# Retention and gated attention with their outputs made channels on partitions, normed by sums over partitions

## The chip, the cores and the metric

The kernel runs on one core of a Trainium2 chip. The metric is the device time of one execution in microseconds (us). TensorE (PE) multiplies; its weight loads are listed apart (PEld). VectorE (DVE), ScalarE (ACT) and GpSimd (POOL) do the elementwise work, and SP, ACT and POOL can issue DMAs.

## The reference, cut to what matters

`x` is 1024 tokens by 1024 channels in f32, and there are two layers. Each projects the normed and modulated `x` to 3088 columns, which are shared out to three groups of heads:

```python
(aq, ak, av, ag, rq, rk, rv, rg, gq, gk, gv, gg, ga) = jnp.split(proj, IN_SPLITS, axis=-1)
a_out = sliding_window_attention(aq, ak, av, sinks) * jax.nn.silu(ag)
r = retention(rq, rk, rv)                        # 4 heads of 64, chunks of 128 tokens
r_out = rms_norm(r) * jax.nn.silu(rg)            # normed over the 64 channels of each head
g = gated_linear_attention(gq, gk, gv, log_a)    # 4 heads, keys of 32, values of 64; log_a from ga
g_out = rms_norm(g, gla_norm_gain) * jax.nn.silu(gg)
y = jnp.concatenate([a_out, r_out, g_out], axis=-1) @ w_out
x = x + gate * rms_norm(y, post_gain)
```

Both recurrent groups work chunk by chunk. With scores `sc` (masked and decayed products of queries and keys) the output of a chunk is `sc @ v`, the part within the chunk, plus `q @ state`, the part from earlier chunks; then `state = decay * state + k^T @ v`.

## The kernel before

Tokens are cut into 8 tiles of 128, handled as `NP_` = 4 pairs. A projection must be as exact as f32, so weights and activations are kept as a high and a low fp32r part, and `accum` sums three products of parts over 8 slices of the 1024 channels: 24 products for a projection. `project` has the activations of one token tile as the stationary operand and up to 272 columns of weights moving, so its result has tokens on partitions. Products of intermediate data (scores, states, transposes) are plain f32, each of which the profile lists as two records.

The input weights come in units of 256 columns, in the order of the table `UNITS`, from DRAM over staging tiles to the arenas; `gg` comes first and carries the 16 columns of `ga`. SP issues most of the DMAs; the letters in `EN` say which engine does a step or issues a DMA (S for SP, A for ACT, G or P for POOL, V for DVE).

A layer runs in this order. `do_gates` projects `gg` and `rg` of each pair, makes SiLU of them (`silu2`: tanh on ACT, one DVE operation) and stores them to DRAM (`sgS`, `srS`). The projections of `ga` go to the job `gla_logits`. Then for each pair of tiles `rq`, `rk` and `rv` are projected and `ret_core` runs; then, in the same manner, gated attention's `gqk`, `gv` and `gla_core`; then attention; then the output projection, which reads the mixed outputs back from `mixS` in DRAM.

In both cores the output of a tile, `po`, has tokens on partitions and 4 heads by 64 columns. The part from the state is a product with 128 stationary columns (the queries), and within the chunk the scores of a head are stationary (128 by 128) and its 64 columns of values move. Then `head_norm_gate` (L988 to L1000) squares `po` on ACT (L990), sums 64 columns per head on DVE, raises to the power of -1/2 in `rstd_of` on POOL (L529), multiplies by it and by the gate on DVE (L995 and the next), has TensorE transpose the two halves (L176), and `store_mix` copies them as high and low parts and stores these to `mixS`.

Only TensorE's order is set by the program itself. Chains of steps are generators, called jobs. `job` starts one, `yield lat(key, l)` says that its next TensorE step may be issued so many microseconds later by a planner's clock `clk`, and `pump`, called between the products of projections, issues the steps that are due; flags such as `("stG", l, t)` carry a time from one job to another. The latencies stand in the table `L` (`hn1` is that from squares to transposes; a name with `@1` is that of layer 1). TensorE runs its instructions in this order whatever the real times are. A scheduler orders the other engines by data and free buffers. Buffers are the pools `t2` (512 columns, `B2` = 12), `t1` (256 columns, `B1` = 8), small ones, and in PSUM `mm` with 3 banks for projections and `aux` with 5 for all the rest. Names in the lists below are these pools' (`t`, `aux`, `mm`), with numbers of a buffer.

The profile shows helpers by their own lines: `mult` is L161, `transp` L176, ACT's copies L145, DMAs L150. L491 makes the low part of a weight, L624 to L628 the high and low parts of the normed input `hT`.

## Time and profile before

| what | us |
|---|---|
| median of 3 runs | 971.86 (971.38 to 972.01) |
| the profiled execution | 971.16 |
| its span from first to last instruction | 969.4 |
| PE busy | 951.3 |
| PEld busy | 829.4 |
| DVE busy | 640.2 |
| ACT busy | 410.1 |
| POOL busy | 272.5 |

The mean granted clock of TensorE was 0.996 of full speed. Times in the rows of the profile are microseconds from the span's start. Busy time counts an instruction from its start to its end, and ends of products on PE are modelled, so one product overlaps the next in the list; the distance from start to next start is what a product costs TensorE.

### The profile page before, as it was taken

The page shows a single profiled execution, that of the slowest core. Times are in us where ns is not written, and L with a number is a line of the kernel's source. Part 1 is how long each engine was busy: PE and PEld are TensorE (multiplying, and loading weights), DVE is VectorE, ACT ScalarE, POOL GpSimd, SP SyncE. Part 2 cuts the span into 40 slices and gives each one's busy share as a digit, 9 for nine tenths or more (in the row PEclk, how much of TensorE's full clock was granted, in tenths as well). Part 3 has the DMA queues.
Part 4 walks back from the last instruction along what each step waited for, and adds up shares of the span by engine and source line. Part 5 has one row for each costly group of instructions (what it writes and reads, how often), then busy time and mean ns, then how long its engine had stood idle before and what let it go on. Part 6 is the DMA issues. An engine that isn't in the chain of part 4 may idle for free.

```text
span 969.4 us, 18061 instructions
## 1 busy us (share of the span) xinstructions
PE 951.3 (98%) x6513; PEld 829.4 (86%) x6513; DVE 640.2 (66%) x1525; ACT 410.1 (42%) x1119; POOL 272.5 (28%) x323
## 2 busy tenths in 40 slices
PE   6999999999999999999999999999999999999997
PEld 1799999989998877878889999998999887777886
DVE  6886857777777777655586485686776577763332
ACT  2777312354422666622455531134652166761111
POOL 3243011533430344511242110144423034441000
PEclk9999999999999999999999999999999999999999
DMA  9943314624335355677455160253222333555871
GB/s 313 320 146 110 111 56 129 187 77 112 115 102 150 98 168 180 218 242 237 172 166 172 50 180 22 83 155 92 80 86 77 120 88 105 158 174 174 261 238 65
DMA packets 124293, 140.30 MB, mean 145 GB/s; under 512 B 12734, under 2 KB 95528, under 8 KB 124204
## 3 DMA queue, kind: packets, MB, share of 16 engines
q1 hardware_dynamic: 116204, 127.43, 42.9%
q10 hardware_dynamic: 8000, 11.72, 3.4%
q8 instruction: 51, 0.84, 0.4%
q14 instruction: 38, 0.31, 0.1%
HBM read 102.42 MB, written 34.60 MB: 141 GB/s over the span
## 4 chain that ended last, share of the span: by engine, by line
PE 86%; DMA 7%; DVE 3%; issue 2%; POOL 1%; ACT 0%; SPq 0%; DVEq 0%; ACTq 0%; POOLq 0%
PE mm L161 67%; PE aux L161 15%; PE aux L176 4%; DMA wm<-in_w_mod_dram 2%; DMA t<-in_x_dram 1%; DMA st<-in_w_in_dram 1%; DMA xk<-in_x_dram 1%; DMA t<-aoS 1%; DMA st<-in_w_mod_dram 1%; POOL sm L529 1%; DVE acc L367 0%; DVE t L1292 0%; POOL arena L491 0%; DVE t L624 0%; DMA c_ident<-cst_ident_dram 0%
## 5 line engine op out<-in xcount | busy, mean ns | idle before, releaser
L161 PE MATMUL mm<-arena,arena 128*128 128x256 f32 (+2 forms) x1896 | 303.0, 315 | 1.4 <-ACT arena L628 0.7
L161 PE MATMUL mm<-arena 128*128 128x256 f32 (+2 forms) x1824 | 294.7, 317 | 0.0
L161 PEld LDWEIGHTS mm<-arena,arena 128*128 128x128 f32 x1896 | 261.8, 188 | 24.6 <-ACT arena L628 1.2
L161 PEld LDWEIGHTS mm<-arena 128*128 128x128 f32 x1824 | 255.4, 191 | 22.0 <-issue 1.2
L161 PE MATMUL mm<-arena,mx 128*128 128x512 f32 (+1 forms) x744 | 168.7, 386 | 0.0
L161 PEld LDWEIGHTS mm<-arena,mx 128*128 128x128 f32 x744 | 135.6, 188 | 29.1 <-issue 1.5
L529 POOL TENSOR_TENSOR sm<-sm,mhalf 128x4 f32<-128x4 f32 (+1 forms) x60 | 51.8, 863 | 294.8 <-DVE sm L528 285.3
L491 POOL TENSOR_TENSOR arena<-st,arena 128x512 fp32r<-128x512 f32 x55 | 80.3, 1467 | 91.3 <-ACT arena L145 34.7
L145 ACT ACTIVATE t<-aux 128x512 f32<-128x512 f32 (+1 forms) x96 | 48.7, 521 | 106.4 <-PE aux L176 44.9
L943 POOL TENSOR_TENSOR smx<-smx,sm 128x512 f32<-128x512 f32 x32 | 36.2, 1131 | 114.8 <-DVE sm L942 111.4
L491 DVE TENSOR_TENSOR arena<-st,arena 128x512 fp32r<-128x512 f32 x65 | 62.3, 969 | 4.7 <-PE mm L161 2.6
L145 ACT ACTIVATE arena<-st 128x512 fp32r<-128x512 f32 x82 | 48.5, 626 | 29.0 <-PE mm L161 13.0
L1247 ACT ACTIVATE t<-mm 128x512 f32<-128x512 f32 x30 | 17.9, 597 | 92.2 <-PE mm L161 40.3
L939 ACT ACTIVATE smx<-smx,sm 128x129 f32<-128x129 f32 x128 | 50.0, 393 | 14.0 <-DVE sm L936 13.9
L1248 DVE TENSOR_TENSOR t<-mm,modg 128x512 f32<-128x512 f32 x30 | 20.6, 689 | 48.6 <-ACT t L1247 48.5
L367 DVE SCALAR_TENSOR_TENSOR acc<-st,c_act,acc 128x512 f32<-128x512 f32 x60 | 47.3, 788 | 7.5 <-DMA st<-in_w_mod_dram 6.8
L1292 DVE SCALAR_TENSOR_TENSOR t<-t,sm,t 128x512 f32<-128x512 f32 x32 | 25.9, 846 | 39.7 <-DMA t<-xs 20.8
L176 PE MATMUL aux<-c_ident,t 128*128 128x128 f32 x288 | 45.5, 278 | 2.9 <-DVE t L602 2.9
L176 PEld LDWEIGHTS aux<-c_ident,t 128*128 128x128 f32 x288 | 34.9, 144 | 7.3 <-DVE t L602 4.2
L934 DVE COPY_PREDICATED smx<-c_curmask,aux 128x256 f32<-128x256 int32 x64 | 25.5, 447 | 15.0 <-ACT smx L145 10.4
L990 ACT ACTIVATE t<-aux 128x256 f32<-128x256 f32 x32 | 12.2, 382 | 54.1 <-PE aux L161 26.8
L995 DVE TENSOR_TENSOR t<-aux,sm 128x256 f32<-128x256 f32 x32 | 13.6, 425 | 30.8 <-POOL sm L529 30.8
(214 smaller groups left out, 1300.9 us busy)
## 6 DMA issues: line engine op xcount, KB each, us to landing
st<-in_w_in_dram SPq DMA_DIRECT2D x96, 256.0 KB
st<-in_w_mod_dram SPq DMA_DIRECT2D x64, 256.0 KB
mx<-mixS SPq DMA_DIRECT2D x30, 512.0 KB
mixS<-t SPq DMA_DIRECT2D x64, 128.0 KB
st<-in_w_out_dram SPq DMA_DIRECT2D x32, 256.0 KB
mixS<-t SPq DMA_DIRECT2D x32, 256.0 KB
wm<-in_w_mod_dram SPq DMA_DIRECT2D x12, 512.0 KB
t<-in_x_dram SPq DMA_DIRECT2D x24, 256.0 KB
```

Source lines behind the costliest of these rows:

```text
L145: A.activation(dst, src, AF.Copy)
L161: T.matmul(dst, lhsT, rhs, start=start, stop=stop)
L176: T.transpose(dst, src, idn)
L367: V.scalar_tensor_tensor(acc, wt, c_act[:, k:k + 1], acc, ALU.mult, ALU.add)
L491: i = (G if first == 0 and kc in LOG else V if first == 0 else eng(f"wlo{kc}")).tensor_tensor(wt[:, 1, 2 * kc:2 * kc + 2, 0:256], st, f(hi ...
L529: after[2] = G.tensor_tensor(r, r, mhalf[:, :w], ALU.pow)
L934: V.copy_predicated(sv, curmask.unsqueeze(1).to_broadcast((P, 2, P)), pv[:, :, n // P - 1, :])
L939: A.activation(sm[:, h, :], sm[:, h, :], AF.Exp, bias=mx[:, h:h + 1], accum_out=sums[:, h:h + 1])
L943: eng("pn").tensor_tensor(sm[:, :, 0:128], sm[:, :, 0:128], rs.unsqueeze(2).to_broadcast((P, 4, P)), ALU.mult)
L1247: A.activation(yg, pm, AF.Square, accum_out=ss[:, nh:nh + 1])
L1248: V.tensor_tensor(yg, pm, modg[l][:, 512 * nh:512 * nh + 512], ALU.mult)
L1292: V.scalar_tensor_tensor(xt[j], yg[j], r, xt[j], ALU.mult, ALU.add)
```

## The change

Outputs, gates and norms of retention and gated attention are made with channels on partitions.

- `rv` takes the first place of `gg` among the units, and with it the 16 columns of `ga`. The values are projected in `do_gates`, stored to a new DRAM buffer `vS` by SP, and loaded back (`lv`, on ACT's queue) when `rq` of the tile is projected. `gg` is projected where `rv` was.
- `project_P` projects the gates with 128 channels of the weights stationary and the 256 tokens of a pair moving; the SiLU of a pair is one tile of 512 columns, stored and loaded as such.
- `within` makes the part within the chunk with the 64 value columns of a head stationary and the scores moving. A head's result takes 64 partitions, two heads fill the two halves, and the four heads and two tiles of a pair fill one PSUM bank `po` [128, 512]. All of it comes ahead of the parts from the state, which have the state stationary and the queries moving, in two products of 128 by 128 per tile.
- `head_norm_gate` runs once per pair. ACT squares and makes the high part (`sqh`), POOL subtracts for the low part (`sql`), two products with the block matrix `bones` (ones where row and column belong to the same head) sum over partitions into `pz`, ACT takes Ln and Exp of -1/2 of it, DVE multiplies with the gate and with `po` (L1007), and the high and low parts are stored. No transposes, no sums on DVE and no powers on POOL are left in it.
- Among the constants `B2` goes from 12 to 13, `B1` from 8 to 9, the low part of `hT` in layer 0 (`hlo0`) from POOL to DVE, `LOG` (weight slices whose low part POOL makes for the first unit) from `(0,)` to `(0, 1, 3)`, and `DH`, `RE` and `FIN`, numbers that place steps of the modulation and the first normed input, from 1 to 0. The table `L` is set anew: `hn1`, now from squares to sums, 8.14 to 4.0 and 10.35 to 4.07 in layer 1; `hn2` 3.76 to 10.19 and 3.59 to 9.0; `rc1` 0.73 to 6.0; `gc5@1` 1.38 to 0.05; `gc4@1` 1.87 to 0.05; and others by less.

```diff
-    ("gg", GG), ("rg", RG),
-    ("rq", RQ), ("rk", RK), ("rv", RV),
+    ("rv", RV), ("rg", RG),
+    ("rq", RQ), ("rk", RK), ("gg", GG),
...
-    sgS = dr.tile([NT, P, 256], F32, name="sgS")
-    srS = dr.tile([NT, P, 256], F32, name="srS")
+    sgS = dr.tile([NP_, P, 512], F32, name="sgS")
+    srS = dr.tile([NP_, P, 512], F32, name="srS")
+    vS = dr.tile([NT, P, 256], F32, name="vS")
...
+    def project_P(pm, l, p, w):
+        h = hT[(l, p)]
+        for t in (2 * p, 2 * p + 1):
+            await_flag(("hT", l, t))
+        for j in range(2):
+            accum(pm[:, 256 * j:256 * j + 256], lambda a, k: w[:, a, k, j * P:j * P + P], lambda b, k: h[:, b, k, 0:256])
...
-    def store_mix(t, kt0, src, n):
...
+    def within(po, i, v, sc):
+        for j in range(2):
+            for r in range(2):
+                h = 2 * j + r
+                mult(po[64 * r:64 * r + 64, 256 * j + P * i:256 * j + P * i + P], v[:, 64 * h:64 * h + 64], sc[:, h],
+                     not i and not j, False, 0.108)
+
+    def head_norm_gate(l, p, po, gate, scale, eps, kt0):
+
+        sq, sh, sl = t2(), t2(F32R), t2(F32R)
         A.activation(sq, po, AF.Square)
-        ss = small(4)
-        V.tensor_reduce(ss, h4(sq), AX.X, ALU.add)
-        r = rstd_of(ss, 4, scale, eps)
-        g1 = t1()
-        V.tensor_tensor(h4(g1), h4(po), r.unsqueeze(2).to_broadcast((P, 4, 64)), ALU.mult)
-        eng("hng").tensor_tensor(g1, g1, gate, ALU.mult)
+        copy("sqh", sh, sq)
+        eng("sql").tensor_tensor(sl, sq, f(sh), ALU.subtract)
         yield lat("hn1", l)
-        pt = aux()
-        for j in range(2):
-            transp(pt[:, j * P:(j + 1) * P], g1[:, j * P:(j + 1) * P], ident)
-        store_mix(t, kt0, pt[:, 0:256].rearrange("p (k q) -> p k q", k=2), 2)
-        flag(("mix", l, t, kt0), lat("hn2", l))
+        pz = aux()
+        mult(pz, bones, sh, True, False)
+        mult(pz, bones, sl, False, True)
+        A.activation(sq, pz, AF.Ln, scale=scale, bias=eps)
+        A.activation(sq, sq, AF.Exp, scale=-0.5)
+        eng("hng").tensor_tensor(sq, sq, gate, ALU.mult)
+        g1 = gate
+        V.tensor_tensor(g1.rearrange("p (t k q) -> p k t q", t=2, k=2), po.rearrange("p (k t q) -> p k t q", t=2, k=2),
+                        sq.rearrange("p (k t q) -> p k t q", t=2, k=2), ALU.mult)
+        copy("mh", sh, g1)
+        V.tensor_tensor(sl, g1, f(sh), ALU.subtract)
+        for a, (k, m) in enumerate((("smh", sh), ("sml", sl))):
+            dma(k, mixS[2 * p:2 * p + 2, :, a, kt0:kt0 + 2, :].rearrange("t p k q -> p t k q"),
+                f(m).rearrange("p (t k q) -> p t k q", t=2, k=2))
+        for t in (2 * p, 2 * p + 1):
+            flag(("mix", l, t, kt0), lat("hn2", l))
...
-        th = t1()
-        after[0] = A.activation(th, pg, AF.Tanh, scale=0.5)
-        sg = t1()
-        after[1] = V.scalar_tensor_tensor(sg, th, 1.0, pg, ALU.add, ALU.mult)
-        return sg
+        th = t2()
+        A.activation(th, pg, AF.Tanh, scale=0.5)
+        V.scalar_tensor_tensor(th, th, 1.0, pg, ALU.add, ALU.mult)
+        return th
...
     def gla_logits(l, t, pg, pa):
         ga = small(16)
         A.activation(ga, pa, AF.Copy)
-        dma("ssg", sgS[t], silu2(pg))
+        v = t1()
+        if EN["rv"] == "A":
+            after[0] = A.activation(v, pg, AF.Copy)
+        else:
+            after[0] = V.tensor_copy(v, pg)
+        dma("ssg", vS[t], v)
         if l == 0:
-            gated[t] = after[0:2]
+            gated[t] = after[0:1]
...
+        po = aux()
+        for c in range(2):
+            within(po, c, vs[c], scz[c])
         for c in range(2):
             t = 2 * p + c
-            v = vs[c]
             if c:
                 yield lat("gc6", l)
             if t > 0:
                 yield (0.0, ("stG", l, t))
-            po = aux()
             if t > 0:
-                mult(po[:, 0:256], qb[:, c * P:(c + 1) * P], stG.rearrange("p h d -> p (h d)"), True, False)
-            for h in range(4):
-                mult(po[:, 64 * h:64 * h + 64], scz[c][:, h], v[:, 64 * h:64 * h + 64],
-                     t == 0, t == 0 or h == 3)
+                for j in range(2):
+                    mult(po[:, 256 * j + P * c:256 * j + P * c + P], stG[:, 2 * j:2 * j + 2, :].rearrange("p h d -> p (h d)"),
+                         qb[:, c * P:(c + 1) * P], False, c == 1 and j == 1)
             if t < NT - 1:
                 V.scalar_tensor_tensor(stC, stC, g[:, c, 24:25], pst[:, 64 * c:64 * c + 64], ALU.mult, ALU.add)
                 eng("stx").tensor_tensor(stG, stC.unsqueeze(1).to_broadcast((P, 4, 64)),
                                          hmask.unsqueeze(2).to_broadcast((P, 4, 64)), ALU.mult)
                 flag(("stG", l, t + 1), lat("gc5", l))
-            job(gla_out(l, t, po[:, 0:256]))
-
-    def gla_out(l, t, po):
-        gate = t1()
-        dma("lsg", gate, sgS[t])
-        yield from head_norm_gate(l, t, po, gate, 1.0 / 64.0, EPS, 6)
+        job(gla_out(l, p, po))
+
+    def gla_out(l, p, po):
+        gate = t2()
+        dma("lsg", gate, sgS[p])
+        yield from head_norm_gate(l, p, po, gate, 1.0 / 64.0, epsc[:, 0:1], 6)
...
+        po = aux()
+        for i, t in enumerate(ts):
+            within(po, i, vs[i], h4(sc[i]))
         for i, t in enumerate(ts):
             if t > 0:
                 yield (0.0, ("stR", l, t))
-            po = aux()
-            for j in range(2):
-                if t > 0:
-                    mult(po[:, j * P:(j + 1) * P], qT[i][:, j * P:(j + 1) * P], stR[:, j, :], True, False)
-                for h in (2 * j, 2 * j + 1):
-                    mult(po[:, 64 * h:64 * h + 64], sc[i][:, h * P:(h + 1) * P], vs[i][:, 64 * h:64 * h + 64],
-                         t == 0, t == 0 or h % 2 == 1)
+            if t > 0:
+                for j in range(2):
+                    mult(po[:, 256 * j + P * i:256 * j + P * i + P], stR[:, j, :], qT[i][:, j * P:(j + 1) * P], False, i == 1 and j == 1)
             if t < NT - 1:
...
         def do_gates(name, p):
             w = unit(l, name)
-            for t in (2 * p, 2 * p + 1):
-                early = l == 0 and name == "gg" and p == 0
+            if name == "rg":
+                pg = mm()
+                project_P(pg, l, p, w)
+                dma("ssr", srS[p], silu2(pg))
+                pump()
+            for t in (2 * p, 2 * p + 1) if name == "rv" else ():
+                early = l == 0 and p == 0
                 pg = begun[t] if early else mm()
                 if early:
                     await_flag(("hT", l, t))
                     complete(t)
-                    job(gla_logits(l, t, pg[:, 0:256], pg[:, 256:272]))
-                elif name == "gg":
+                else:
                     project(pg[:, 0:272], l, t, w, 272)
-                    job(gla_logits(l, t, pg[:, 0:256], pg[:, 256:272]))
-                else:
-                    project(pg[:, 0:256], l, t, w)
-                    dma("ssr", srS[t], silu2(pg[:, 0:256]))
+                job(gla_logits(l, t, pg[:, 0:256], pg[:, 256:272]))
                 pump()
             if p == NP_ - 1:
-                load(l, "rk" if name == "gg" else "rv")
-            if name == "gg" and p % 2:
+                load(l, "rk" if name == "rv" else "gg")
+            if name == "rv" and p % 2:
...
+        if l == 0:
+            bt = t1()
+            G.memset(bt[:, 0:P], 0.0)
+            for r in range(2):
+                G.memset(bt[64 * r:64 * r + 64, 64 * r:64 * r + 64], 1.0)
+                G.memset(epsc[:, r:r + 1], (EPS, 4.0 * EPS)[r])
+            A.activation(bones, bt[:, 0:P], AF.Copy)
         await_flag("tables")
         for p in range(NP_):
             last = p == NP_ - 1
             rr = {}
-            for name in ("rq", "rk", "rv"):
+            for name in ("rq", "rk"):
                 w = unit(l, name)
                 for tt in range(2):
                     t = 2 * p + tt
+                    if name == "rq":
+                        v = rr[("rv", tt)] = t1()
+                        dma("lv", v, vS[t])
                     pm = mm()
                     project(pm[:, 0:256], l, t, w)
-                    src = pm[:, 0:256]
-                    if name == "rv":
-                        v = t1()
-                        copy("rv", v, src)
-                        rr[("rv", tt)] = v
+                    rr[(name, tt)] = ret_rot(t, pm[:, 0:256], qdec if name == "rq" else kdec)
+                    if name == "rk":
                         job(ret_turn(l, t, rr[("rq", tt)], rr[("rk", tt)]))
                         if tt:
                             job(ret_core(l, p, [rr[("rk", i)] for i in range(2)], [rr[("rv", i)] for i in range(2)]))
-                    else:
-                        rr[(name, tt)] = ret_rot(t, src, qdec if name == "rq" else kdec)
                     pump()
                 if last:
-                    load(l, {"rq": "gqk", "rk": "gv", "rv": "kv"}[name])
+                    load(l, {"rq": "gqk", "rk": "gv"}[name])
+            pg = mm()
+            project_P(pg, l, p, unit(l, "gg"))
+            dma("ssg", sgS[p], silu2(pg))
+            pump()
+            if last:
+                load(l, "kv")
...
-B2, B1, BS, BST, MMB, SMB = 12, 8, 11, 5, 3, 6
+B2 = 13
+B1 = 9
+BS, BST, MMB, SMB = 11, 5, 3, 6
...
-DH = 1
-RE = 1
+DH = 0
+RE = 0
...
-LOG = (0,)
+LOG = (0, 1, 3)
...
-FIN = 1
+FIN = 0
```

The order on PE around the first pair of retention in layer 0, before. `arena` are weights and `hT`, `stR` is the state, `t` are queries, keys, scores and values; `128x64` is the output's shape, and `x` the count in a row:

```order
L161 MATMUL aux_1538<-t_234_1413,t_248_1502 128x64 x4
L161 MATMUL aux_1543<-t_234_1413,t_224_1340 128x128 x2
L161 MATMUL mm_1522<-arena_356,arena_71 128x256 x10
L161 MATMUL mm_1584<-arena_71 128x256 x21
L161 MATMUL aux_1607<-stR,t_242_1465 128x128
L161 MATMUL aux_1607<-t_238_1448,t_249_1503 128x64 x2
L161 MATMUL aux_1607<-stR,t_242_1465 128x128
L161 MATMUL aux_1607<-t_238_1448,t_249_1503 128x64 x2
L161 MATMUL aux_1614<-t_238_1448,t_229_1377 128x128 x2
L161 MATMUL mm_1584<-arena_71 128x256 x3
```

And now:

```order
L161 MATMUL aux_1512<-t_229_1475,t_181_1170 64x128 x4
L161 MATMUL aux_1512<-t_230_1476,t_197_1243 64x128 x4
L161 MATMUL aux_1521<-t_181_1170,t_205_1310 128x128 x2
L161 MATMUL mm_1495<-arena_357,arena_71 128x256 x10
L161 MATMUL mm_1547<-arena_71 128x256 x21
L176 MATMUL aux_1571<-c_ident,t_226_1463 128x128 x4
L161 MATMUL aux_1512<-t_222_1436,stR 128x128 x2
L161 MATMUL aux_1582<-t_197_1243,t_210_1347 128x128 x2
L161 MATMUL mm_1547<-arena_71 128x256 x3
L161 MATMUL mm_1608<-arena_71 128x256 x24
L161 MATMUL mm_1645<-arena_71,arena_357 128x256 x14
L161 MATMUL aux_1660<-t_249_1591,bones 128x512
L161 MATMUL aux_1660<-t_250_1592,bones 128x512
```

The four value products of the second tile moved up to those of the first, the two tiles share `aux_1512`, the products with the state follow 31 projection products later, and the sums with `bones` another 41 products on. The same engine in gated attention of layer 1, second pair, before (`stG` is the state, `sc` the scores):

```order
L161 MATMUL mm_8663<-arena_71 128x256 x7
L161 MATMUL aux_8671<-stG,t_1526_8511 128x256
L161 MATMUL aux_8671<-t_1514_8442,sc_8060 128x64 x4
L161 MATMUL mm_8663<-arena_71 128x256 x14
L161 MATMUL aux_8705<-stG,t_1526_8511 128x256
L161 MATMUL aux_8705<-t_1522_8489,sc_8061 128x64 x4
L161 MATMUL mm_8663<-arena_71 128x256 x3
```

And now:

```order
L161 MATMUL mm_8278<-arena_71 128x256 x14
L161 MATMUL aux_8293<-sc_7760,t_1324_8111 64x128 x4
L161 MATMUL aux_8293<-sc_7761,t_1326_8138 64x128 x4
L161 MATMUL aux_8293<-t_1331_8171,stG 128x128 x2
L161 MATMUL mm_8278<-arena_71 128x256 x7
L161 MATMUL aux_8293<-t_1331_8171,stG 128x128 x2
L161 MATMUL mm_8278<-arena_71 128x256 x3
```

Between the two products with `stG`, the second of which needs the state that DVE makes from the first chunk, there stood four value products and 14 projection products, and there stand 7 projection products. On ACT, at the second pair of retention in layer 0, the norm and its loads now read:

```order
L150 DMA t_292_1890<-srS 128x512
L996 ACTIVATE t_293_1892<-aux_1809 128x512
L145 ACTIVATE t_294_1893<-t_293_1892 128x512
L150 DMA t_313_2024<-vS 128x256
L1003 ACT_TABLE_LOAD
L1003 ACTIVATE t_293_1892<-aux_1949,epsc 128x512
L461 ACTIVATE t_306_1965<-aux_1960 128x512
L1004 ACT_TABLE_LOAD
L1004 ACTIVATE t_293_1892<-t_293_1892 128x512
```

Where one square of 256 columns per tile stood, with copies and a tanh behind it, there are now a square and a copy of 512 columns per pair and, later, Ln and Exp, each behind a load of its table.

40 lines of the change are left out of this document (16 added, 24 removed).

## The prediction

> **What bounds the kernel now.** I read the engines' busy times, then the chain that ended last, then what TensorE waited for, then busy time by stretch.
>
> ```profile
> span 969.4 us, 18061 instructions
> PE 951.3 (98%) x6513; PEld 829.4 (86%) x6513; DVE 640.2 (66%) x1525; ACT 410.1 (42%) x1119; POOL 272.5 (28%) x323
> PE 86%; DMA 7%; DVE 3%; issue 2%; POOL 1%; ACT 0%; SPq 0%; DVEq 0%; ACTq 0%; POOLq 0%
> ```
> ```profile
> PE aux L176 <- DVE posr L408: 6.2, 1, 6.2
> PE aux L176 <- DVE t L602: 2.9, 2, 2.5
> PE mm L161 <- ACT arena L628: 0.7, 2, 0.5
> PE aux L161 <- DVE t L1209: 0.4, 1, 0.4
> ```
> ```profile
> 110.00:205.00 95.00, 94.38 (x766) 89.35 (x765) 63.52 (x179) 25.77 (x55) 25.85 (x30) 1.00 0.35 106
> 205.00:300.00 95.00, 94.83 (x739) 88.04 (x739) 74.63 (x206) 40.64 (x106) 31.24 (x44) 1.00 0.42 123
> 655.00:755.00 100.00, 100.00 (x804) 93.67 (x803) 69.86 (x204) 45.28 (x118) 39.25 (x57) 1.00 0.28 85
> ```
>
> TensorE is busy 98% of the span and 86% of the chain. Its two long waits (6.2 and 2.9 us) lie in the first 20 us, under the loads of `w_mod`. In retention and gated attention (110 to 300 us, and 570 to 755 us in layer 1; columns: stretch, PE, PEld, DVE, ACT, POOL, clock, DMA) it never idles for more than a few tenths, while ACT is busy 27 to 45% and POOL 27 to 39%. So the time here is the number of TensorE instructions times their pitch; work on other engines counts only if it makes TensorE wait. Busy times overlap, so I price TensorE by start to next start.
>
> **TensorE, removed and added.** A retention tile, a transpose pair and a gated-attention tile in the timeline of PE (start, busy, instruction):
>
> ```profile
> 121.67 0.38 PE L161 MATMUL aux<-stR,t 128*128 128x128 f32 x2
> 121.89 0.56 PE L161 MATMUL aux<-t,t 128*128 128x64 f32 x4
> 122.29 0.44 PE L161 MATMUL aux<-stR,t 128*128 128x128 f32 x2
> 122.56 1.06 PE L161 MATMUL aux<-t,t 128*128 128x64 f32 x8
> 123.38 3.09 PE L161 MATMUL mm<-arena 128*128 128x256 f32 x24
> ...
> 127.10 0.38 PE L176 MATMUL aux<-c_ident,t 128*128 128x128 f32 x2
> 127.24 0.95 PE L161 MATMUL mm<-arena,arena 128*128 128x256 f32 x6
> ```
> ```profile
> 226.53 0.59 PE L161 MATMUL aux<-stG,t 128*128 128x256 f32 x2
> 226.96 1.00 PE L161 MATMUL aux<-t,sc 128*128 128x64 f32 x8
> 227.77 2.09 PE L161 MATMUL mm<-arena 128*128 128x512 f32 x8
> ```
>
> One f32 product is two records. Scores times values costs 0.81 us a tile (226.96 to 227.77; in retention 0.40 for half a tile, and half of the 0.82 that holds the new state's four records as well). 32 tiles: 26.0 us. State products: retention 0.22 + 0.27 = 0.49, gated attention 0.43, each for 14 tiles: 12.9 us. Transposes: 32 pairs by 0.14 = 4.5 us. Removed: 43.4 us.
>
> Added, first the state products, all in retention's form with the operands exchanged: 28 tiles by about 0.46 (the mean of 0.49 and 0.43) = 12.9 us. Then scores times values with 64 stationary columns and 128 moving ones, alternating between the two column halves. No such product is in the trace; the nearest are attention's values (64 columns, 256 moving) and retention's scores (half the rows, 128 moving):
>
> ```profile
> 332.07 1.08 PE L161 MATMUL aux<-t,va 128*64 128x256 f32 x8
> 332.98 0.60 PE L161 MATMUL aux<-t,vd 128*64 128x256 f32 x4
> 333.51 1.65 PE L161 MATMUL aux<-kT,mx 64*128 64x128 f32 x24
> ```
> ```profile
> 113.47 1.16 PE L161 MATMUL aux<-t 64*128 64x128 f32 x16
> 114.56 2.27 PE L161 MATMUL mm<-arena,arena 128*128 128x256 f32 x17
> ```
>
> Two tiles are 16 records. By half of attention's pitch (1.44 us for 12 records of 256) they take 0.96 us, by the scores 1.09, and with no overlap of the halves 1.62 as now. I take 1.10, near the two, since entering and leaving such a group is not in the pitch: 16 groups by 1.10 = 17.6 us, ends 15.4 and 26.0. Last the sums over partitions: two fp32r products of 512 columns per pair of tiles, 32 in all, at the 163.0 us of 696 in
>
> ```profile
> L161 PE MATMUL mm<-arena,mx 128*128 128x512 f32 x696 | 163.0, 393 | 0.0
> ```
>
> = 7.5 us. Added: 12.9 + 17.6 + 7.5 = 38.0. TensorE saves 5.4 us, between 7.6 and -3.0. The projections keep their number: two token tiles by 24 products of 256 columns become two channel halves by 24 of 256, and the 16 columns of `ga` move from `gg` to `rv`: zero, as both forms stream 256 columns.
>
> [...]
>
> **The other engines.** Norm chain and its prices:
>
> ```profile
> L145 ACT ACTIVATE t<-aux 128x512 f32<-128x512 f32 x64 | 36.7, 590 | 65.4 <-PE aux L161 39.2 <-PE aux L176 13.4 <-issue 6.6
> L628 ACT ACTIVATE arena<-t 128x512 fp32r<-128x512 f32 x28 | 17.4, 637 | 10.3 <-DVE t L624 10.2
> L990 ACT ACTIVATE t<-aux 128x256 f32<-128x256 f32 x32 | 12.2, 382 | 54.1 <-PE aux L161 26.8 <-DVE t L825 17.8 <-PE mm L161 6.3
> L491 POOL TENSOR_TENSOR arena<-st,arena 128x512 fp32r<-128x512 f32 x55 | 80.3, 1467 | 91.3 <-ACT arena L145 34.7 <-PE mm L161 29.6 <-DMA sgS<-t 15.6
> L529 POOL TENSOR_TENSOR sm<-sm,mhalf 128x4 f32<-128x4 f32 x32 | 35.1, 1097 | 152.7 <-DVE sm L528 149.1 <-DVE gs L1081 3.3
> L995 DVE TENSOR_TENSOR t<-aux,sm 128x256 f32<-128x256 f32 x32 | 13.6, 425 | 30.8 <-POOL sm L529 30.8
> L1106 DVE TENSOR_TENSOR t<-t,t 128x512 f32<-128x512 f32 x8 | 6.3, 786 | 0.0
> ```
> ```profile
> 114.21 0.63 ACT L1038 ACTIVATE t<-t 128x512 f32<-128x512 f32 x1
> 114.85 1.28 ACT L1039 ACT_TABLE_LOAD   x1
> 114.95 0.34 ACTq L150 DMA_DIRECT2D t<-srS  x1
> 116.15 0.63 ACT L1039 ACTIVATE t<-t 128x512 f32<-128x512 f32 x1
> ```
>
> ACT loses 96 instructions of 256 columns (32 each of square, high part and tanh, about 0.38: 36 us), gains 96 of 512 (square, its high part, Ln, Exp, high part, tanh, about 0.61: 59 us), 30 table loads (38 us) and 8 more loads to issue (24 for 16, at 0.34: 3 us): +64, to about 474 us of 970. It stays under TensorE in every stretch. DVE loses five instructions of 256 columns or less per tile and branch and the gates' product; it gains three of 512 columns per pair and 14 splits of `hT` from POOL: some 15 us less. POOL loses 35.1 us of powers and those 14 splits, and gains 16 subtractions of up to 1.47. Moving `rv` ahead adds 16 stores on SP, where 32 fewer stores of the mixed output and 24 fewer of gates more than pay, and 16 loads on ACT's queue, behind which Tanh and the copies wait for a free buffer. None of this is on the path while TensorE's order leaves room.
>
> Room at the sums: from the last state product to the first sum lie 24 to 41 projections, 3 to 5 us. What must happen: square 0.59, high part 0.64, subtraction 1.47, with hand-overs about 2.9. It fits, with 0.1 to 2 us to spare. After the sums two table loads, Ln, Exp and two DVE products (1.28 + 0.59 + 1.28 + 0.63 + 0.79 + 0.7 = 5.3 us) hold one of the five small PSUM banks; other banks are free for that while. Tightest is layer 1's state of gated attention: three times 7 projections (0.85 us) where 14 with four value products stood, against the end of the product before (0.28) and the state's update on DVE,
>
> ```profile
> L1164 DVE TENSOR_TENSOR stG<-stC,c_hmask 128x256 f32<-128x256 f32 x14 | 6.3, 448 | 1.5 <-PE aux L161 1.4
> ```
>
> 0.45. DVE is at 70% there, so half an instruction more, 0.2 to 0.3, will often stand ahead: I take 0.3 by 3 = 0.9 us of new waits, ends 0 and 5 (0.3 at all 16 groups). The start's changes (`DH`, `RE`, `FIN`, `LOG`, split of `hT` on DVE) can win back at most the 0.7 us that TensorE waits for `hT`, and may lose as much; I take a gain of 0.4.
>
> **Sum.** The profiled execution took 971.16 us, its span and 1.7 around it; the median of the runs is 971.86, 0.7 more. 971.16 - 5.4 + 0.9 - 0.4 = 966.3, which stands at 967.0 beside the median. Without new waits and with the cheapest products: 971.86 - 7.6 - 0.7 = 963.6.
>
> **Rivals.**
>
> [...]
> 2. No change: waits eat the 5 us. ACT works in order, and Ln and Exp with their loads hold back copies that empty TensorE's banks: 1.28 + 0.59 + 1.28 + 0.63 = 3.8 us in a piece, 16 times. If 0.35 us of each reaches TensorE, the time is about 972. For it: ACT at 43% with waits on PE; against it: three banks for projections, each 2.9 us of products.
> 3. Slower: the sums come too early. The subtraction stands on POOL behind two weight splits of 1.47 in several places. With two of these still to run, the chain is 5.8 us against 3 to 5, and TensorE, in order, waits 0.8 to 2.8; everything behind waits too. It is slower than before by over 0.2% from a mean of 0.43 us over the 16 sums; at 0.8 it gives 967 + 13 = 980. Against it: POOL is idle over 60% of every stretch.
> 4. Slower by price: column halves don't overlap; 971.86 + 3.0 = 974.9. Against it: attention's rows.
>
> **Chances.** Less than 0.2% (1.9 us around 971.86) cannot be told from no change. Forecast (963.6 to 969.9) 0.50; rival 1 0.22; rival 2 0.14; rival 3 0.10; rival 4 0.04. So faster 0.72, same 0.14, slower 0.14. The forecast's own range is 963.6 to 969.9. For 8 in 10 I leave out the lowest part of rival 1 and most of 3 and 4: 959.5 to 974.
>
> **What would show it.** In the changed profile: value products with 64 columns at about 0.55 us a tile; 32 products with `bones` at 0.23; no pairs of transposes behind the heads; PE still at 98% with waits on DVE and ACT under 3 us from 110 us on; 41 table loads with ACT under 50%. I am wrong if PE waits at the sums (on POOL), at `stG` (on DVE) or for a bank, or if the 64-column products are priced as the old ones.

## The result, and the profile after

The changed kernel took 979.95 us (median of 7, 974.50 to 982.56) where the kernel before took 971.86 (median of 7); the ratio is 1.0072, 95% interval 1.0056 to 1.0089. It is slower; the forecast was 967.0 with a range to 974. Its executions fall into two groups, 974.5 to 975.0 us and 978.6 to 982.6, and the profiled one, at 975.02, is of the lower, so the trace shows only part of the loss: its span is 3.9 us longer than that of before. The page's first lines, and what TensorE (PE) waited for (in total, times, longest):

```profile
span 973.3 us, 17739 instructions
PE 946.5 (97%) x6509; PEld 817.5 (84%) x6509; DVE 636.7 (65%) x1412; ACT 468.5 (48%) x1149; POOL 242.6 (25%) x296
PE 81%; DVE 5%; DMA 5%; ACT 5%; issue 2%; POOL 1%; SPq 0%; DVEq 0%; POOLq 0%; ACTq 0%
```
```profile
PE aux L176 <- DMA wm<-in_w_mod_dram: 5.8, 1, 5.8
PE aux L176 <- DVE t L610: 5.2, 2, 3.7
PE aux L161 <- DVE t L1226: 1.8, 3, 1.1
PE aux L176 <- ACT t L145: 1.7, 1, 1.7
PE aux L176 <- DVE smx L944: 1.5, 2, 1.0
PE aux L161 <- ACT mx L1139: 1.4, 1, 1.4
PE aux L176 <- DVE t L1195: 1.0, 1, 1.0
```

The first, at the kernel's start, was there before too (6.2 us); the second was 2.9; the others are new or grown. TensorE is busy 4.8 us less, and idle 8.7 us more. By stretch (PE busy is the second number, PEclk the third from the end), first before, then after:

```profile
0.00:50.00 50.00, 40.16 (x193) 23.94 (x194) 37.52 (x84) 24.93 (x61) 13.32 (x27) 0.93 0.92 307
50.00:300.00 250.00, 248.46 (x1988) 235.17 (x1987) 186.01 (x501) 105.40 (x257) 75.25 (x89) 1.00 0.40 119
300.00:400.00 100.00, 99.50 (x612) 78.39 (x612) 76.26 (x143) 60.76 (x191) 40.36 (x40) 1.00 0.48 143
570.00:755.00 185.00, 185.00 (x1513) 175.48 (x1512) 130.64 (x374) 64.89 (x158) 54.85 (x70) 1.00 0.31 90
```
```profile
0.00:50.00 50.00, 37.20 (x158) 20.79 (x159) 35.95 (x75) 21.91 (x55) 14.46 (x26) 0.90 0.91 306
50.00:300.00 250.00, 249.84 (x2028) 233.79 (x2027) 186.99 (x455) 137.15 (x278) 62.34 (x79) 1.00 0.42 129
300.00:400.00 100.00, 96.80 (x595) 76.16 (x594) 76.61 (x141) 60.44 (x191) 38.41 (x40) 1.00 0.46 138
570.00:755.00 185.00, 180.21 (x1498) 166.77 (x1497) 126.52 (x316) 93.41 (x172) 47.65 (x61) 1.00 0.33 99
```

Idle grew by 3.0 us in the first 50 us, by 2.7 where attention begins, and by 4.8 in layer 1's retention and gated attention; it fell by 1.8 in the rest. In layer 0's retention and gated attention, the place of the same edit, TensorE waits less than before. The new products cost what was forecast, or less (timeline of PE):

```profile
125.87 0.61 PE L161 MATMUL aux<-t,stR 128*128 128x128 f32 x4
126.31 0.61 PE L161 MATMUL aux<-t,t 128*128 128x128 f32 x4
...
131.60 0.63 PE L161 MATMUL aux<-t,bones 128*128 128x512 f32 x2
132.07 1.10 PE L161 MATMUL mm<-arena,arena 128*128 128x256 f32 x8
...
224.00 1.09 PE L161 MATMUL aux<-sc,t 128*64 128x128 f32 x16
225.03 3.92 PE L161 MATMUL mm<-arena 128*128 128x512 f32 x16
```

A group of 16 value records takes 1.03 us from start to next start (forecast 1.10), a pair of sums 0.47 (0.468), a tile's two state products 0.44. TensorE is nevertheless only 4.8 us less busy, because of its clock: behind the first waits it is granted at half (0.50 from 21 to 26 us).

```profile
18.00:24.00 6.00, 5.63 (x22) 2.65 (x20) 6.00 (x12) 1.90 (x4) 2.47 (x3) 0.72 1.10 341
36.00:40.00 4.00, 4.00 (x22) 4.00 (x21) 3.81 (x14) 3.98 (x11) 0.24 (x1) 0.58 0.95 284
```
```profile
18.00:27.00 9.00, 5.77 (x20) 3.50 (x21) 8.07 (x15) 1.46 (x3) 5.25 (x5) 0.62 1.07 361
40.00:44.00 4.00, 4.00 (x22) 4.00 (x22) 4.00 (x13) 3.60 (x10) 1.72 (x3) 0.59 0.81 252
```

Before (first pair of lines), twice 3.4 us at half clock: 6 us at 0.72, 4 at 0.58. After (second pair), 6.8 and 3.3. The 3.4 us more at half clock lose, by estimate (half of 3.4), up to 1.7 us of work, which the busy time hides: without them TensorE is busy some 6.5 us less, against the 5.4 forecast. Two later profiles of the same kernel bear this out: with 6.8 us at half clock in the start, as before, TensorE is busy 943.5 and 944.3 us, 7.8 and 7.0 less than before.

### The profile page after: what moved, and what is told of

Read it like the earlier page. It is cut to its first block, busy times and chain, and to the rows that moved or that the text cites. A ratio compares the mean times of both kernels' runs of the same rounds, so it can differ in the third digit from the quotient of the medians.

```text
span 973.3 us, 17739 instructions
## 1 busy us (share of the span) xinstructions
PE 946.5 (97%) x6509; PEld 817.5 (84%) x6509; DVE 636.7 (65%) x1412; ACT 468.5 (48%) x1149; POOL 242.6 (25%) x296
## 4 chain that ended last, share of the span: by engine, by line
PE 81%; DVE 5%; DMA 5%; ACT 5%; issue 2%; POOL 1%; SPq 0%; DVEq 0%; POOLq 0%; ACTq 0%
PE mm L161 66%; PE aux L161 12%; PE aux L176 4%; DMA st<-in_w_mod_dram 2%; DVE acc L368 1%; DMA wm<-in_w_mod_dram 1%; ACT t L145 1%; DVE arena L492 1%; ACT smx L949 1%; ACT L1003 1%; ACT mx L1139 1%; DMA c_ones<-cst_ones_dram 0%; DMA t<-aoS 0%; ACT mx L1138 0%; DMA rows<-in_b_mod_dram 0%
## 5 line engine op out<-in xcount | busy, mean ns | idle before, releaser
L492 POOL TENSOR_TENSOR arena<-st,arena 128x512 fp32r<-128x512 f32 x57 | 84.1, 1481 | 139.6 <-PE mm L161 62.4
L145 ACT ACTIVATE t<-aux 128x512 f32<-128x512 f32 x64 | 36.6, 588 | 92.3 <-PE aux L161 43.9
L537 POOL TENSOR_TENSOR sm<-sm,mhalf 128x1 f32<-128x1 f32 x30 | 18.3, 611 | 181.8 <-DVE sm L536 178.5
L998 POOL TENSOR_TENSOR t<-t,t 128x512 fp32r<-128x512 f32 x16 | 21.7, 1356 | 117.9 <-ACT t L145 106.7
L176 PE MATMUL aux<-c_ident,t 128*128 128x128 f32 x224 | 35.1, 285 | 6.3 <-DVE t L610 5.2
L944 DVE COPY_PREDICATED smx<-c_curmask,aux 128x256 f32<-128x256 int32 x64 | 25.6, 447 | 17.1 <-ACT smx L145 13.2
L176 PEld LDWEIGHTS aux<-c_ident,t 128*128 128x128 f32 x224 | 27.5, 146 | 9.8 <-DVE t L610 6.5
L145 ACT ACTIVATE t<-t 128x512 fp32r<-128x512 f32 x32 | 20.2, 632 | 18.9 <-DVE t L1007 18.5
```

The costliest lines, as they stand in the source:

```text
L145: A.activation(dst, src, AF.Copy)
L176: T.transpose(dst, src, idn)
L492: i = (G if first == 0 and kc in LOG else V if first == 0 else eng(f"wlo{kc}")).tensor_tensor(wt[:, 1, 2 * kc:2 * kc + 2, 0:256], st, f(hi ...
L537: after[2] = G.tensor_tensor(r, r, mhalf[:, :w], ALU.pow)
L944: V.copy_predicated(sv, curmask.unsqueeze(1).to_broadcast((P, 2, P)), pv[:, :, n // P - 1, :])
L998: eng("sql").tensor_tensor(sl, sq, f(sh), ALU.subtract)
```

## Experiments

Ratios are to runs of the kernel before on the same chip, with 95% intervals; 1% is 9.7 us. The kernel before took 971.2 to 972.2 us on these chips, and the changed kernel's executions spread, so differences between chips are taken from the ratios. `after` is the changed kernel; a second set of seven of its executions, further below, gives 1.0062 instead of 1.0072.

### The start

```diff
 after, start constants of before
-DH, RE, FIN = 0; LOG = (0, 1, 3); "hlo0": "V"
+DH, RE, FIN = 1; LOG = (0,); "hlo0": "G"
```

> The changed kernel with five start constants of the kernel before (DH, RE, FIN = 1, LOG = (0,), hlo0 on POOL); all else as changed. Theory 1: in the changed kernel's profile TensorE's first long wait ends at 23.2 us instead of 19.1, since RE = 0 sends the root of the mean square past DVE and then to POOL; with the old constants the start comes back: 4 to 6 us less than the changed kernel (974 to 976 where that takes 980), its runs spread over about 4 us instead of 8, mean granted clock 0.996. Theory 2: the start's delay is chance of the first loads, and the loss sits in waits between 300 and 740 us: no change, 978 to 980. Theory 3: both starts are equal but the new constants suit the new order of loads: 2 us or more slower than the changed kernel.

974.74 us, 1.0042 (1.0028 to 1.0056): 5.2 us less than the changed kernel by the medians, 2.9 by the ratios. That is theory 1 by its time, but by the ratio the kernel still loses 4.1 us to the one before, and its executions still spread over 5.8 us.

The opposite, the five constants of the change in the kernel before:

> The kernel before with the changed kernel's five start constants (DH, RE, FIN = 0, LOG = (0, 1, 3), hlo0 on DVE) and nothing else. Theory 1: slower than before by 4 to 6 us (976 to 978), with TensorE's second wait ending at about 23 us. Theory 2: the same as before within 0.2%.

976.21 us, 1.0040 (1.0028 to 1.0053), with the second wait ending at 22.9 us: theory 1. So about half of the loss has nothing to do with outputs, gates or norms. Then one constant alone:

```diff
 after
-RE = 0
+RE = 1
```

> The changed kernel with RE = 1 alone, so that the early root of the mean square stays on POOL after ACT's sums, as before; the other start constants as changed. Theory 1a (RE alone makes the first transposes late): all of the 5 us that the five constants gave, 974 to 976. Theory 1b (RE holds only the 2 to 3 us of TensorE's two first waits, and the rest of the five is DH and LOG, which make the first weights and hT late): 976.5 to 978.5. Rival: 979 to 981, RE does nothing.

972.67 us, 1.0023 (1.0004 to 1.0042): by the ratios 4.8 us less than the changed kernel, so `RE` alone gives back no less than all five did. Whether the other four are a gain or a loss is not shown, since the two intervals overlap. In the kernel before, `RE = 0` alone:

> The kernel before with RE = 0 alone. With RE = 1 the changed kernel lost 7 us, more than the 5 of all five constants together. If RE is the whole of the start's loss and does the same in either kernel: 4 to 7 us slower than before, 976 to 979, as with all five constants (976.2). Rival (RE costs only in the changed kernel, by what stands around it there): within 2 us of before.

974.83 us, 1.0026 (1.0016 to 1.0036): the same sign, 2.5 us, less than expected and more than the rival's 2, where all five constants cost 3.9. With `RE = 1` POOL makes all three small steps of the root of the mean square right behind ACT's sums. With `RE = 0` the root goes over two small DVE instructions to POOL (L537) and back, and the small DVE ones stand behind products of 512 columns. POOL and DVE after, at the two first transposes:

```profile
18.12 1.05 POOL L537 TENSOR_TENSOR sm<-sm,mhalf 128x1 f32<-128x1 f32 x1 [14.40 <-DVE sm L536]
20.63 0.99 POOL L537 TENSOR_TENSOR sm<-sm,mhalf 128x1 f32<-128x1 f32 x1 [1.46 <-DVE sm L536]
...
19.21 0.88 DVE L610 TENSOR_SCALAR t<-xk,sm 128x512 f32<-128x512 f32 x2 [0.44 <-POOL sm L537]
21.66 1.88 DVE L610 TENSOR_SCALAR t<-xk,sm 128x512 f32<-128x512 f32 x2 [0.45 <-POOL sm L537]
```

Before, the scaled rows (L602) were done at 18.0 and 19.5 us. The transposes wait 3.7 and 1.5 us instead of 2.5 and 0.4, and TensorE stays at half clock for 3.4 us more: 2.3 + 1.7 = 4.0. The share of the clock varies: in the two later profiles of the changed kernel these waits are 6.2 and 6.6 us in all, 3.3 and 3.7 more than before, with no more time at half clock than before.

### The table loads

```diff
 after
-        A.activation(sq, pz, AF.Ln, scale=scale, bias=eps)
-        A.activation(sq, sq, AF.Exp, scale=-0.5)
+        A.activation(sq, pz, AF.Copy)
+        A.activation(sq, sq, AF.Copy)
```

> The changed kernel with copies of the same size in place of Ln and Exp, so that the output isn't normed, and the 30 added table loads of 1.28 us are gone. Theory 1 (the later waits, 1.7 at 335 us, 1.4 at 737, 0.5 at 683, come from ACT, which does its work in order behind two loads per norm): 2 to 4 us less than the changed kernel, table loads back at 11, ACT at about 430 us. Rival: the later waits come from DVE's products (L1005, L1007) ahead of the scores' masks and from the program's new order of TensorE: less than 1 us.

979.51 us, 1.0064 (1.0045 to 1.0082): no gain beyond the interval, which is the rival by its size, though ACT is busy 40 us less and the two waits in gated attention (1.4 and 0.5) are gone. Both edits together:

> The changed kernel with both edits: the old start constants, and copies in place of Ln and Exp (the output isn't normed). Theory 1: the two gains add, 6 to 10 us less than the changed kernel, 970 to 974: then start and table loads hold most of the loss and TensorE's saved 5 us shows. Rival: 976 or more, and the loss sits elsewhere.

975.06 us, 1.0033 (1.0020 to 1.0045): neither theory nor rival, and within the intervals no more than the start's part. The profile of the first of these two, of an execution that took 979.88, shows why, and what a wait costs. Waits of TensorE, DVE and POOL in layer 1's retention, and three stretches:

```profile
PE aux L161 <- DVE t L1226: 6.1, 3, 4.0
```
```profile
645.46 0.43 DVE L147 CAST arena<-st 128x512 fp32r<-128x512 f32 x1
...
656.37 1.82 DVE L368 SCALAR_TENSOR_TENSOR acc<-st,c_act,acc 128x512 f32<-128x512 f32 x1 [2.75 <-DMA st<-in_w_mod_dram]
658.12 3.54 DVE L147 CAST arena<-st 128x512 fp32r<-128x512 f32 x1
...
664.28 0.69 DVE L1005 TENSOR_TENSOR t<-t,t 128x512 f32<-128x512 f32 x1
665.00 0.69 DVE L1007 TENSOR_TENSOR t<-aux,t 128x512 f32<-128x512 f32 x1
666.39 0.69 DVE L1010 TENSOR_TENSOR t<-t,t 128x512 fp32r<-128x512 f32 x1 [0.70 <-ACT t L145]
667.00 1.41 DVE L1226 TENSOR_TENSOR t<-aux,c_causal 128x256 f32<-128x256 f32 x4
```
```profile
657.58 3.79 POOL L793 MEMSET mx<- 128x512 f32 x8
```
```profile
642.00:664.00 22.00, 21.48 (x158) 19.34 (x156) 18.06 (x32) 7.31 (x13) 11.12 (x13) 1.00 0.40 123
664.00:668.00 4.00, 0.53 (x4) 0.49 (x6) 3.27 (x8) 1.29 (x3) 0.00 (x0) 0.71 0.93 290
668.00:672.00 4.00, 4.00 (x24) 3.58 (x22) 0.59 (x3) 0.00 (x0) 0.00 (x0) 0.50 0.65 219
```

DVE waits 2.75 us for a load of `w_mod`; then its CAST, 0.43 at 645.46, lasts 3.54 beside eight clears on POOL; then, with other work, three steps of the norm (L1005, L1007, L1010) stand ahead of the masks of the scores (L1226), for which the value products wait 4.0 us. And TensorE then runs at half clock for 6.8 us, which by estimate (half of 6.8) costs up to 3.4 more. So one wait of 4.0 us was worth some 7.4 at most. (Another of 1.9 us at 636 us, also on L1226, drew 3.4 us at half clock.) The CAST ends 0.3 us after the last clear (661.66 and 661.37).

This row is not alone. In the kernel with both edits and in the one with the late value products (below) the same CAST meets the clears too, and takes 3.54 and 5.25 us:

```profile
653.35 3.54 DVE L147 CAST arena<-st 128x512 fp32r<-128x512 f32 x1
658.04 5.25 DVE L147 CAST arena<-st 128x512 fp32r<-128x512 f32 x1
```

Each ends 0.3 us after the last clear, which ends at 656.61 and 663.00. In the three profiles of the changed kernel itself the CAST begins 1.2 to 1.5 us before the clears, and takes 1.51 us (beside another POOL instruction), 0.41 and 2.43. DVE's products were not held up in this way: in the changed kernel's first profile those beside the clears keep their length, 0.69 us (POOL first, then DVE).

```profile
655.38 4.07 POOL L793 MEMSET mx<- 128x512 f32 x8
655.76 0.69 DVE L492 TENSOR_TENSOR arena<-st,arena 128x512 fp32r<-128x512 f32 x1
```

So a shift of 1 to 2 us in that part of the kernel can decide whether this CAST takes 0.4 or 5 us. The stretches at half clock come in two lengths: in 17 of the 20 profiles, from 0 to 960 us, there are 35 of them (by windows of 2 us), 26 of 3.4 us and 9 of 6.8.

### The clears

```diff
 gla_tiles, in after (L793) and in before (L783)
-                    G.memset(z_[:, 512 * q:512 * q + 512], 0.0)
+                    A.activation(h4(z_[:, 512 * q:512 * q + 512]), ident.unsqueeze(1).to_broadcast((P, 4, P)),
+                                 AF.Copy, scale=0.0)
```

> The changed kernel with the eight clears of gated attention's tiles on ACT instead of POOL, nothing else; TensorE's order is the same. Theory 1 (the upper group of executions, 979 to 982, is the clears' 4 us wait in layer 1): the upper group goes, 974 to 976. Theory 2 (the upper group comes from the start, where RE = 0 makes the first transposes late): no change, 978 to 981 with both groups.

976.16 us (974.76 to 978.60), 1.0053 (1.0037 to 1.0068): none of 6 executions is above 979, where 6 of the changed kernel's 15 were. That speaks for theory 1, but the ratio has not moved beyond the intervals of 1.0072 and 1.0062. With `RE = 1` too:

> The changed kernel with RE = 1, and with the eight clears of gated attention's two tiles (L793, 3.8 us in a row on POOL at 653 to 661 us in layer 1) made on ACT; TensorE's order is the same to the row. Theory (DVE's work of 512 columns takes up to 3.5 us instead of 0.4 while POOL clears, and this makes the scores' masks of retention's last pair late): the wait on L1226 of 1.2 to 4.0 us at 659 to 667 us goes, 1 to 3 us less than the 972.7 with RE = 1, and its upper runs (976 to 978) go. Rival (DVE is late there from its own work and from the load of w_mod): within 1 us.

972.88 us (971.01 to 975.33), 1.0013 (1.0004 to 1.0022): the four executions of 976 to 978 among twelve with `RE = 1` alone are gone, the median stays, as the rival has it. The wait on L1226 was still 1.4 us. In the kernel before:

> The kernel before with the same clears on ACT; TensorE's order is the same. Theory (before, the masks of that pair are not due while POOL clears): within 0.7 us of before. Rival: the clears cost in either kernel, 1 us or more less.

973.14 us, 1.0017 (1.0009 to 1.0026): 1.7 us slower, and neither the theory nor the rival. In the profile of before no CAST falls beside the clears, and the masks beside them keep their length, so there was nothing to win; that ACT's eight instructions are what costs is likely, and no run shows it apart. With the copies in place of Ln and Exp as well:

> The changed kernel with RE = 1, the clears on ACT, and copies in place of Ln and Exp (the output isn't normed): table loads and clears no longer hold back DVE or ACT in layer 1. Theory (TensorE's saved 5 us come out once these waits are gone): 967 to 970, faster than before. Rival (the waits move on to the next step that DVE makes): 971 to 975.

971.46 us, 0.9997 (0.9986 to 1.0008). Against 972.88 on the same chip the table loads now show, 1.4 us, with intervals that overlap a little. But TensorE's 6 us don't come out, which is the rival; 1.9 us of waits on L1226 and 1.7 at attention's start are left.

Two more profiles of the changed kernel, taken to catch one of its executions above 978 us:

> The changed kernel once more, one profile. Its executions fell into two groups, 974.5 to 975.0 and 978.6 to 982.6; the profile at hand is of the lower. If this one is of the upper, it shows where the 4 to 6 us between them lie. Theory 1: in the first 45 us (loads of w_mod and the first weights). Theory 2: in layer 1's retention, at the wait on the masks of its last pair (1.1 us in the profile at hand, 4.0 in one of the kernel without table loads).

> The changed kernel as it is. If the profiled execution takes 978 us or more: theory 1, a wait of 3 to 4 us on the masks (L1226) at 660 to 668 us with a CAST of 3.5 us on DVE beside the clears, and TensorE at half clock for 3.4 or 6.8 us behind it; theory 2, longer waits and more half clock in the first 45 us than the 10.2 us at half clock of the first profile. If it takes 974 to 976, neither is told apart and this stays argued.

The first took 973.93 us, and the second 974.64; the second's seven executions took 973.79 to 982.89 (median 977.38, ratio 1.0062, 1.0037 to 1.0087). Both profiles took under 975 us, so no trace of this very kernel shows what its longer executions have. What all 15 executions have is their mean clock: six of 973.8 to 975.0 us had 0.994 to 0.996; of nine at 977.4 and above, eight had 0.987 to 0.992. If all of the loss is half clock, 0.991 over 980 us is 17.6 us at half speed, where 0.994 is 11.7: by this estimate the longer ones had some one to four more such stretches of 3.4 us. Which wait sets them off there is argued, from the kernel without table loads and from what moving the clears did; it is not shown.

### The order of TensorE

The second tile's value products put back behind the first tile's state:

```diff
 ret_core, after with the start constants of before
-        for i, t in enumerate(ts):
-            within(po, i, vs[i], h4(sc[i]))
         for i, t in enumerate(ts):
             if t > 0:
                 yield (0.0, ("stR", l, t))
+            within(po, i, vs[i], h4(sc[i]))
```

> The changed kernel with the old start constants, and in retention the value products of the second tile of a pair put back behind the first tile's state update, where they stood before. Theory (in layer 1 these products come before DVE has masked the second tile's scores, since DVE holds weight splits and the norm's products there): the waits on the masks (L1226), 1.1 us at 633 to 660 us in the profiled execution and up to 6 in others, go; 1 to 3 us less than the 974.7 of the kernel with the old start constants. Rival (DVE is simply late in that stage, and TensorE meets it at the next step that needs DVE): within 1 us.

981.55 us, 1.0099 (1.0083 to 1.0115), 5.5 us slower by the ratios instead of 1 to 3 faster. Waits on L1226 rose from 1.1 to 3.5 us, and TensorE was busy 3.8 us more: value products of one tile alone took 0.59 us from start to next start (median), half of a pair's group 0.51, and a tile's state products behind them 0.55 instead of 0.45. Theory and rival both fell. In this profile the CAST of 5.25 us beside the clears also stands ahead of the masks, so not all of the loss need come from the order. Raised latencies:

```diff
 table L, after with the start constants of before
-"rc3@1": 2.6, "gc2@1": 2.24, "aq3": 11.35
+"rc3@1": 5.5, "gc2@1": 4.0, "aq3": 13.0
```

> The changed kernel with the old start constants and three latencies of the planner raised, which move TensorE's steps back: rc3 of layer 1 from 2.6 to 5.5 (scores to value products), gc2 of layer 1 from 2.24 to 4.0 (to gated attention's transposes), aq3 from 11.35 to 13.0 (softmax to its transposes, layer 0). Theory (the later waits stem from steps that stand too early in TensorE's order): waits of 1.1 on the masks, 1.9 in gated attention and 2.2 in attention shrink, 970.5 to 973. Rival (other steps become late in their place): 974 to 976.

977.06 us, 1.0056 (1.0043 to 1.0069), 1.4 slower by the ratios, with overlapping intervals: no gain, as the rival has it. The waits on the masks and on L1139 went and attention's shrank from 2.2 to 1.4; others took their place:

```profile
PE aux L176 <- DVE t L1195: 2.7, 1, 2.7
PE aux L161 <- ACT t L1145: 2.6, 1, 2.6
...
PE aux L161 <- DVE t L1007: 1.5, 1, 1.5
```

Of the three, the one in layer 0 alone, on top of `RE = 1` and clears on ACT:

> The changed kernel with RE = 1 and the clears on ACT, and aq3 of layer 0 from 11.35 to 13.0, which moves attention's transposes after the softmax eight products or so back. Theory (the 1.5 to 1.9 us at 334 us come from transposes that stand too early, while ACT waits in order for the copies of queries from DMA): 1 to 2 us less than 972.9. Rival: the same wait is met at the value products: no change.

971.79 us, 1.0000 (0.9991 to 1.0009): 1.1 less, with intervals that overlap a little, and level with the kernel before. In the profile without it, TensorE waited there 1.77 us at 333.5, and the clock fell to half behind it (4 us at 0.57):

```profile
333.00:337.00 4.00, 3.50 (x13) 3.17 (x14) 2.66 (x7) 2.58 (x9) 0.64 (x1) 0.57 0.23 80
```

It is not a matter of length alone: 1.66 us in the changed kernel's first profile and 1.86 in the second, at the same place, were not followed by half clock. One latency more, to let ACT make copies ahead of Ln and Exp:

```diff
 head_norm_gate, the kernel above
-        yield lat("hn1", l)
+        yield lat("hn1", l) + (1.5 if l and kt0 == 6 else 0.0)
```

> The changed kernel with RE = 1, the clears on ACT, aq3 at 13.0, and the latency before the sums of gated attention in layer 1 raised by 1.5 us, by which ACT makes the last pair's copies (L1138, L1139) ahead of Ln and Exp. Theory: the wait of 1.4 us at 734 us goes or shrinks to the 0.5 us of the other pairs, 970.6 to 971.3 where before takes 971.5: faster than before by 0 to 0.1%. Rival: the copies of keys (L1145) behind the same Ln and Exp are late in their place: 971.5 to 972.5, no gain.

976.80 us, 1.0049 (1.0033 to 1.0066), 5 slower; the rival, and worse than it said. The keys' copies (L1145) fell behind the loads in three places, 1.3 us each, with half clock behind one of them (3.4 us from 721 us on):

```profile
PE aux L161 <- ACT t L1145: 4.4, 4, 1.3
```
```profile
696.70 1.28 ACT L1003 ACT_TABLE_LOAD   x1
698.00 0.69 ACT L1003 ACTIVATE t<-aux,epsc 128x512 f32<-128x512 f32 x1
698.70 1.28 ACT L1004 ACT_TABLE_LOAD   x1
700.00 0.63 ACT L1004 ACTIVATE t<-t 128x512 f32<-128x512 f32 x1
700.53 0.36 ACT L1145 ACTIVATE t<-aux 128x256 f32<-128x256 f32 x1
```

Buffers, 14 of 512 columns instead of 13, and 7 of 256 instead of 9:

```diff
 after with RE = 1 and clears on ACT
-B2, B1 = 13, 9
+B2, B1 = 14, 7
```

> The changed kernel with RE = 1 and the clears on ACT, and with 14 buffers of 512 columns instead of 13 (and 7 of 256 instead of 9); TensorE's order is the same. Theory (in layer 1 a mask of the last retention pair waits for a buffer whose gate, stored to DRAM by SP, lands 3.1 us after its issue): the wait on L1226 at 660 us goes, 0.5 to 1.5 us less than 972.9. Rival: another wait takes its place, or seven of the small buffers are too few: no change or slower.

985.60 us, 1.0142 (1.0123 to 1.0161), the rival. The wait on L1226 went, but TensorE waited 9.5 us in four pieces, up to 4.0, for retention's rotated queries and keys (L1195), with half clock behind two of them (mean clock 0.988). That the lack of small buffers made these late is likely, and was not tried apart. Last, more sums:

```diff
 head_norm_gate, after with the start constants of before
-        mult(pz, bones, sl, False, True)
+        mult(pz, bones, sl, False, False)
+        mult(pz, bones, sl, False, False)
+        mult(pz, bones, sl, False, True)
```

> The changed kernel with the old start constants and with each product of bones and the squares' low part done three times (the sums take the low part three times): 32 more fp32r products of 512 columns. If TensorE bounds the time and a sum costs 0.23 us, 32 by 0.23 = 7.4 us more, 981 to 983. Rival (TensorE has slack at the sums, since it waits for other engines a little later anyway): 1 to 5 us more, 976 to 980.

984.20 us, 1.0127 (1.0113 to 1.0142), 8.3 us more by the ratios. Four products took 0.93 us, so 32 more are 7.5: the first theory. TensorE bounds the time, and has no slack at the sums.

## Why the prediction was wrong

- **TensorE's sum was right.** Forecast 5.4 us less; by pitch, 16 groups by 1.03, 16 pairs of sums by 0.46 and 28 state products at 12.6 in all are 36.5 against the 38.0 put in, so 6.9 less (16.5 + 7.4 + 12.6), and the busy time says 6.5 to 7.8 where the clock's part is out. The column halves overlap nearly as attention's do (1.03 us, where half of attention's pitch gave 0.96). A saving of 10.0 us, with value products at half of their cost before, stands behind the 0.22 of rival 1 and the range's lower end of 959.5; no run shows such a halving: a group took 1.03 us, where 16 records took 1.62 before. ACT's load was right too: 41 table loads and 468.5 us against 474. DVE's was not: it fell by 3.5 us, and not by some 15.
- **The start's term failed.** "I take a gain of 0.4" from `DH`, `RE`, `FIN`, `LOG`, with a bound of 0.7 us, was the wait for one edge of `hT`; the step left out what `RE` puts between ACT's sums and the first transposes. `RE` cost 2.5 us in the kernel before and, by the ratios, 4.8 in the changed one.
- **New waits were put at 0.9 us, with 5 as the end, and at the wrong places.** They were looked for at the sums (no wait on the squares' parts in the changed kernel's profile) and at the state of gated attention (none in the changed kernel's profile). They came at the masks of retention in layer 1, at its keys, at attention's transposes, and in gated attention behind Ln and Exp: 7.5 us in layer 1 and attention. Rival 2 had the last of these (1.9 us), which went with the table loads. The step "none of this is on the path while TensorE's order leaves room" failed: the order has no room left at these places. At the masks the rows show why, pieces of the norm of 0.7 us each and a long CAST ahead of them on DVE; what holds up the keys and attention's transposes, and what the new table `L` has to do with it (three of its latencies were tried; it also takes `rc1` of layer 1 from 0.12 to 6.0 and `mod4` from 5.8 to 0.39), stays open.
- **A wait was priced at its own length.** 1.3 to 4.0 us of waiting drew 3.4 or 6.8 us at half clock behind it, though not each time, and by estimate up to half of that is lost. The profile before the change has such stretches in its first 50 us (0.93 in the row above), and the prediction passed over them.
- Rival 3's time (980) came true by none of its mechanism: POOL's subtractions were in time.
- The way back, in ratios: 1.0072, and 1.0062 when repeated; clears on ACT 1.0053; `RE = 1` too 1.0013; attention's transposes later 1.0000. Only the step of `RE` is clear of the intervals. Why TensorE, busy 6.8 us less than before, then only reaches level is seen in that profile in waits of 1.4 (L1139), 1.2 (L1226), 1.0 (L1195) and 1.7 us (L944), and one of 2.7 for a load of `w_mod` in the start. No version beat the kernel before beyond its interval.

## What to carry to other kernels

When one engine is busy 98% of the time in an order fixed by hand, count a change of its work as a gain only after checking, at each place where it waits for another engine, what will newly stand ahead of the work it waits for; a list of constants that come with a change is to be priced one by one. Price a wait of TensorE with the half clock that may follow: here waits of 1.3 to 4.0 us drew 3.4 or 6.8 us of it, though not each time. And undo the parts singly, and against the repeated kernel: a part with no effect alone (the table loads) had some when another wait was gone, and a kernel whose executions spread over 9 us gives differences of medians that its ratios do not bear out.

## What was not expected of the hardware

- TensorE's clock halved in pieces of 3.4 us (26 of 35 stretches; the other 9 were 6.8), some of them behind waits as short as 1.28 us (0.33 of another just before it) or 1.77 us in the middle of a busy program, and not always (1.86 us was not followed by it): the same kernel's executions spread over 9 us, the longer ones with less of the clock (0.987 to 0.996).
- A CAST of 512 columns on DVE took 3.54 us, twice, and 5.25 once, instead of 0.4, beside eight clears on POOL, while DVE's products of two inputs beside such clears kept their 0.69.
- A table load was 1283 ns, and the next instruction began within 20 ns of its end (696.70, 698.00); Ln and Exp in turn took 28 loads for 16 norms.
- A group of 64-column products cost 0.16 us more when it was split in two (2 by 0.59 against 1.02), and the state products behind it 0.55 instead of 0.45.
